# Moving the output gate's projection to block products, and forming the forget gates' low weight halves by adding transfers

## The chip, the cores and the metric

The kernel runs on one core of one Trainium2 chip. The time is the device time of one execution in microseconds (us). The core has five engines that work side by side, each with its own queue in fixed order: TensorE (PE, matrix products into PSUM), VectorE (DVE), ScalarE (ACT), GpSimd (POOL) and SyncE (SP, which here only issues transfers). Transfers between the chip's main memory and the core's memory (SBUF) are issued by SP, ACT or POOL.

## The reference

One layer of a hybrid backbone is applied to 640 tokens of width 1024: 128 context tokens and 512 latent tokens. After a modulation of the input, one wide projection feeds everything:

```python
h = x * (1.0 + scale1) + shift1
proj = h @ p['w_in']
q, f_fwd, f_bwd, i_raw, g_raw, hy, mg = jnp.split(proj, SPLIT_IDX, axis=-1)
o_a, s_f, s_b = hgrn2_mixer(q, f_fwd, f_bwd, i_raw, g_raw, lb, p['hgrn_norm_w'], s0_fwd, s0_bwd)
o_b = hyena_mixer(hy, p, row_len)
```

`hgrn2_mixer` is a gated linear recurrence in both directions over 8 heads of 128 channels. `f_fwd` and `f_bwd` are its forget gates, `i_raw` its values, `g_raw` its output gate:

```python
o = o * lax.rsqrt(jnp.mean(jnp.square(o), axis=-1, keepdims=True) + RMS_EPS) * norm_w.astype(f32)
o = o.reshape(bsz, L, D_A) * jax.nn.silu(g_raw.astype(f32))
```

`hyena_mixer` is a long convolution. Both branches are gated (`mg`), mixed, projected and normalised; a feed-forward block with its own normalisation follows.

## The kernel before

**Two halves of each number.** Each fp32 operand of a large product is split into a rounded high half and the rest, the low half. A product is then three matrix products (`PASSES`): high x high, high x low, low x high. A weight tile of 1024 x 128 is loaded as `raw`, cast on ACT or DVE to the high half `wh`, and the low half `wl` is `raw` minus `wh` (`issue`, line 346; the subtraction is line 358, on DVE, on POOL for some of the first eight tiles). Three buffers each exist for `raw`, `wh` and `wl`, and `advance` (line 361) prepares up to two tiles ahead of the one in use. The strings `HIE` and `LOOK` hold one letter per tile of this stream: the engine of the cast, and how far to look ahead.

**Dense products.** `dense_fm` (line 607) multiplies one 1024 x 128 tile with 320 of the 640 tokens: 8 blocks of the inner dimension x 3 passes. Both halves of the tokens make 48 products of 320 columns for one tile of 128 output channels.

**Block products.** The class `Wino` (line 623) computes two output tiles at once for both token halves by a 2 x 2 block scheme with 7 block products instead of 8. A block product is 4 inner blocks x 3 passes, so a pair costs 84 products instead of 96. In exchange DVE forms sums of weight blocks (`rest`, line 648) and sums of results. In the first projection stage this serves the pairs in `M1_ORDER`: the convolution's `x0`, the mixing gates `mga` and `mgb`, the queries `q` and one pair of forget gates `f`, 14 pairs in all. Its order is written out in `PLAN`: the token `g5` loads and splits the first weight tile of pair 5, `w5` the second one and the sums, `15` to `75` are its seven block products. `m1_done` (line 817) adds the results, applies the gate's function, and stores each finished tile to the scratch `sd` in main memory; line 842 holds a case for an output gate `g`. Tokens `Q` and `Z` put the modulation's own products (`ada`) between them.

**Stages in time.** First the filters and `start`; then the block products, up to about 310 us of the profiled span; then the convolution; then, from about 564 us, the recurrence; then the projection of its output (`pa`), the output product (`wo`), the feed-forward block, and its output (`fo`) to the end.

**The recurrence** follows the order in `HGSEQ`. For head `h`, `a` and `b` are its two forget gates (`hg_f`, line 1146), `q` and `g` its query and output gate, `e` the elementwise part (`hg_elem`, line 1165) and `s` the scan and its norm (`hg_scan`, `hg_post`). `hg_unit` (line 1321) turns each token into a unit of work: a tile that `M1_ORDER` holds is loaded from `sd` (`qg_load`, `f_load`), any other is a dense product with a weight tile from the stream. Seven heads have their forget gates as dense products, all eight their output gates. Between a head's `e` and `s` stand the next head's `a b q g`. The `mga` tiles that are not in `M1_ORDER` come after the last `s` in this order.

`hg_elem` takes the logarithm of the gate on ACT, runs prefix sums on DVE, exponentials on ACT and a row of products on DVE. Its large tiles `t4` to `t7` have one buffer each, as has the gate's own tile `sg` (tag `t1`). `hg_scan` begins with the transposes `kT` on PE, which read the result of these products, then forms scores (`sc`, `scp`), masks them on DVE, and multiplies (`u`, `o`).

The order of instructions in each engine's queue is fixed when the program is built: the library goes by the order in the source and by its own estimate of when an instruction's operands are ready, so that a later piece of work can be placed into a gap. Casts and low halves have priority there.

Of the kernel before, what the change touches and what calls it, by code (L numbers as in the profile page):

```python
# [13 lines left out]
ALU = mybir.AluOpType  # L14
# [3 lines left out]
P = 128  # L18
# [19 lines left out]
COL_Q, COL_FF, COL_FB, COL_I, COL_G = 0, 1024, 2048, 3072, 4096  # L38
# [77 lines left out]
    return {k: np.ascontiguousarray(v) for k, v in c.items()}  # L116


PLAN = """x0 k0 L0 k1 x4 k2 p mlp t L1 T0 x3 T4 A0 x2 D0 T2 A1 x1 L2 B0 M0 T1 D2 A2 M2 T3 h0 L3 B1 D1 A3 h1 B2 M1 D3 h2 h3 M3 h4 W2 W0 h5 h6 h7 W1 q V0 e0 B3 g0 W3 V1 m w0 e2 10 20 g1 50 11 60 g2 70 21 30 40 w1 w2 61 51 52 12 71 Q8 62 22 g3 w3 13 41 g4 53 72 Q9 42 31 63 w4 g5 23 14 w5 73 Z4 Q10 43 32 g6 w6 64 24 15 54 74 Q11 33 65 25 44 16 26 55 75 Q12 Z5 g7 34 w7 66 45 56 17 76 Q13 35 67 46 g8 27 57 w8 18 77 Z6 Q14 g9 g10 36 w9 28 19 68 37 29 58 78 Q15 69 47 59 w10 79 Q16 38 110 210 Z7 g11 610 49 111 510 39 48 w11 211 g12 611 112 w12 212 710 Q17 g13 511 711 Q18 410 113 w13 311 612 Z8 310 411 512 712 Q19 513 213 613 412 713 312 413 313 Z9"""
HMOD = "SVSSVSSS"  # L120
HSUB = "GVVVVGVG"
WSUB = "VGGVVGGG"
# [2 lines left out]
HFE = "VSVSVSVS" * 3 + "VSVSVSVS" + "VSSSVSSS"  # L125
XSE = "S" * 24
M1PRI = 99
M1_ORDER = (('mgb', 6, 7), ('f', 0, 1), ('mgb', 4, 5), ('x0', 6, 7), ('mgb', 2, 3), ('mga', 4, 5), ('x0', 4, 5), ('q', 0, 1), ('q', 2, 3), ('x0', 2, 3), ('q', 6, 7), ('q', 4, 5), ('x0', 0, 1), ('mga', 6, 7))
FFNP = "1-1 2-1 g1 w1"
FFNT = ("g2", "", "")  # L130
FFN0 = "51 61 12 22 w2 71"
PERIOD = (("g", 1), ("w", 1), ("6", 0), ("1", 1), ("4", -1), ("5", 0), ("7", 0), ("3", -1), ("2", 1))
WPRI = 2
HIE = """SSSSVVSVSVSSSSSSSVVVSVVSVSSVSSSSSSSSSSSSSSSSSSSSSSSSSSSSSSSSSSSSSSSSSSSSSSSSSSSSSSSSSSSSSSSSSSSSSSSSSSSSSSSSSS"""
LOOK = """22222012202102201120122111222222222222222222222222222222222222222222222222222222222222222222222222222222222222"""
CONVSEQ = """a0 b0 c0 d0 e0 a1 b1 c1 f0 d1 e1 a2 b2 f1 s04 c2 s00 d2 x0 p0 s01 e2 i00 s02 a3 i01 s03 b3 i02 i03 f2 o00 c3 d3 e3 o01 a4 f3 s14 x1 s10 b4 c4 p1 s11 d4 i10 s12 e4 a5 i11 s13 b5 c5 d5 i12 f4 i13 o10 e5 a6 o11 f5 b6 s24 x2 s20 p2 s21 c6 i20 d6 s22 e6 i21 s23 a7 b7 i22 i23 c7 o20 f6 d7 o21 m0 e7 f7 s34 s30 n0 x3 m1 p3 s31 i30 s32 i31 s33 n1 i32 i33 o30 o31"""
HGSEQ = """a0 b0 q0 g0 e0 v2 v3 a1 b1 q1 g1 s0 e1 a2 b2 q2 g2 s1 e2 a3 b3 q3 g3 s2 e3 a4 b4 q4 g4 s3 e4 a5 b5 q5 g5 s4 e5 a6 b6 q6 g6 s5 e6 a7 b7 q7 g7 s6 e7 s7 c m0 m1 t m2 m3 p0 m4 p1 m5 p2 m6 p3 m7 p4 p5 p6 p7"""
PHB = 2
# [24 lines left out]
def body(tc, I, O):  # L163
    nc = tc.nc
    V, S, G, PE, SY = nc.vector, nc.scalar, nc.gpsimd, nc.tensor, nc.sync
# [3 lines left out]
    def act(out, in_, func, bias=0.0, scale=1.0):  # L169
        r = S.activation(out, in_, func, bias=bias, scale=scale)  # L170
        if func in TABLE_FUNCS:
            if last_table[0] is not None:
                tc.add_manual_dep(
                    r.ins, last_table[0].name,
                    mybir.DependencyInfo(mybir.DependencyClass.NoSync, mybir.DependencyReason.DATA),
                    reason="table order")
            last_table[0] = r.ins
        return r

    def tt(out, a, b, op, eng=None):  # L180
        return (eng or V).tensor_tensor(out=out, in0=a, in1=b, op=op)  # L181
# [4 lines left out]
    def f32(ap):  # L186
        return ap.bitcast(F32)
# [29 lines left out]
    def mm_bank(nm):  # L217
        return bank("mm", nm)
# [20 lines left out]
    w1 = sp.tile([EMB, ORD], F32, name="w1")  # L239
# [12 lines left out]
    w2 = sp.tile([P, ORD], F32, name="w2")  # L252
    w3 = sp.tile([P, 2, ORD], F32, name="w3")
# [84 lines left out]
    stream = dict(specs=[], hl=[], pos=0, stop=None)  # L338

    def w_fm(wap, col):  # L340
        return (wap.rearrange("(k p) n -> p k n", p=P)[:, :, col:col + P], (KT, P), None)

    def w_tm(wap, k0, nk, col, ncol, own=None):
        return (wap.rearrange("(k p) n -> p k n", p=P)[:, k0:k0 + nk, col:col + ncol], (nk, ncol), own)

    def issue(i):
        src, (a, b), own = stream["specs"][i]
        raw = wp.tile([P, a, b], F32, tag="raw", bufs=RAW_BUFS, name=f"raw{i}")
        SY.dma_start(raw, src)
        if own is None:  # L350
            q, th, tl, n = wp, "wh", "wl", HL_BUFS
        else:
            q, th, tl, n = own[0]["p"], "wbh", "wbl", own[1]
        hi = q.tile([P, a, b], F32R, tag=th, bufs=n, name=f"wh{i}")
        lo = q.tile([P, a, b], F32R, tag=tl, bufs=n, name=f"wl{i}")
        with tc.high_priority():
            (V.tensor_copy if HIE[i] == "V" else S.copy)(hi, raw)  # L357
            tt(lo, raw, f32(hi), ALU.subtract, G if i < len(WSUB) and WSUB[i] == "G" else V)
        stream["hl"].append((hi, lo))

    def advance(pos, n):
# [6 lines left out]
        end = len(specs) if stream["stop"] is None else stream["stop"]  # L368
        while ns < end and look < int(LOOK[pos]) and live < HL_BUFS and specs[ns][2] is None:
            ns += 1  # L370
# [15 lines left out]
    def U(fn, *specs):  # L386
        units.append(Unit(list(specs), fn))
# [219 lines left out]
    def dense_fm(w, x, half, ps, kt=KT, after=None):  # L607
        c0 = half * HT
        for k in range(kt):
            for i, (a, b) in enumerate(PASSES):  # L610
                r = PE.matmul(ps[:, 0:HT], w[a][:, k, :], x[b][:, k, c0:c0 + HT],  # L611
                              start=k == 0 and i == 0, stop=k == kt - 1 and i == 2)
                if k == 0 and i == 0:
                    order_after(r, after)
        return r
# [97 lines left out]
    w_in = I["w_in"][0]  # L713
    def v_add(p):
        U(v_unit(p), w_tm(w_in, 0, 4, COL_I + p * 256, 256), w_tm(w_in, 4, 4, COL_I + p * 256, 256))
# [6 lines left out]
    def start():  # L722
# [42 lines left out]

        for tok in PLAN.split():
            if tok == "mlp":
# [9 lines left out]
    M1 = []  # L777
    for kind, a, b in M1_ORDER:
        M1.append(tuple((kind, t) for t in (a, b)))
# [266 lines left out]
    def gate_add(j, tag):  # L1046
        col = COL0[tag] + j * P
        U(gate_unit(j, tag), *(() if (tag, j) in slot else (w_fm(w_in, col),)))
# [73 lines left out]
    def hg_qg(h, which):  # L1122
        def fn(w):
            o = hg["p"].tile([P, T], F32, tag=which, bufs=2 if which == "g" else 1, name=f"{which}{h}")
            for half in range(2):
                cs = slice(half * HT, half * HT + HT)
                ps = mm_bank(f"{which}{h}_{half}")
                dense_fm(w, hT, half, ps)
                act(o[:, cs], ps[:, 0:HT], AF.Sigmoid)
                if which == "g":  # L1130
                    V.scalar_tensor_tensor(o[:, cs], ps[:, 0:HT], norm_w, o[:, cs], ALU.mult, ALU.mult)
                else:
                    tt(o[:, cs], ps[:, 0:HT], o[:, cs], ALU.mult)
            hg[which, h] = o
        return fn

    def qg_load(h, which):
        hg[which, h] = hg["p"].tile([P, T], F32, tag=which, bufs=2 if which == "g" else 1, name=f"{which}{h}")
        spilled(which, h, hg[which, h])

    def f_load(h):
        hg["k", h] = hg["p"].tile([P, 2, T], F32, tag="t1", bufs=1, name=f"sg{h}")
        for d in range(2):
            spilled("f", 2 * h + d, hg["k", h][:, d])

    def hg_f(h, d):
        def fn(w):
            if d == 0:
                hg["k", h] = hg["p"].tile([P, 2, T], F32, tag="t1", bufs=1, name=f"sg{h}")
            o = hg["k", h]  # L1150
            for half in range(2):
                ps = mm_bank(f"f{d}_{h}_{half}")
                dense_fm(w, hT, half, ps)
                act(o[:, d, half * HT:half * HT + HT], ps[:, 0:HT], AF.Sigmoid)
        return fn
# [165 lines left out]
    def hg_unit(tok):  # L1321
        op, h = tok[0], int(tok[1:] or 0)
        if op in "ab":
            d = "ab".index(op)
            if ("f", 2 * h) in slot:
                if d == 0:
                    U(lambda: f_load(h))
                return
            U(hg_f(h, d), w_fm(w_in, (COL_FF, COL_FB)[d] + h * P))
        elif op in "qg":  # L1330
            if (op, h) in slot:
                U(lambda: qg_load(h, op))
            else:
                U(hg_qg(h, op), w_fm(w_in, COL0[op] + h * P))
        elif op == "s":
            U(lambda: (hg_scan(h), hg_post(h)))
        elif op == "e":
            U(lambda: hg_elem(h))
        elif op == "v":
            v_add(h)  # L1340
        elif op == "m":
            gate_add(h, "mga")
        elif op == "p":
            U(proja_unit(h), w_fm(I["proj_a"][0], h * P))
        else:
            U(dict(c=lambda: comb_open(), t=hg_tail)[op])
# [34 lines left out]
    for tok in HGSEQ.split():  # L1381
        hg_unit(tok)
# [402 lines left out]
```

## Time and profile before

| | us |
|---|---|
| median of 3 runs | 1434.0 |
| lowest and highest | 1432.09, 1435.02 |
| the profiled execution | 1434.2 |
| its span | 1431.9 |

A profile is one execution. Its page gives each engine's busy time, the waits, and groups of instructions; the trace behind it can be asked for single instructions. A row of a group reads: line, engine, operation, written tile <- read tiles, shapes, how many | busy us in all, mean ns of one | idle time of the engine just before them, and what ended it. A row of the timeline reads: start, length, engine, line, operation, tiles, shapes, count, and in brackets the engine's idle time before it with what ended it. A row of the stretch view reads: stretch, its length, then for each engine its busy us and the count of its instructions, then the granted share of PE's clock, the busy share of the transfer engines, and GB/s.

```profile
L181 DVE TENSOR_TENSOR wl<-raw,wh 128x1024 fp32r<-128x1024 f32 x96 | 117.3, 1224 | 134.8 <-ACT wh L357 131.2
L357 ACT CAST wh<-raw 128x1024 fp32r<-128x1024 f32 x90 | 94.1, 1049 | 221.8 <-PE pb L611 41.0
```

These two groups are the low halves on DVE (line 181 is the helper `tt` through which most of DVE's two-operand work goes) and the casts on ACT, over the whole kernel. PE's granted clock was 1.00 in every stretch that is quoted below.

### The profile page before, as it was taken

To read this page: it belongs to the slowest core of one execution; us is meant where nothing else is said; L and a number is where in the kernel's file an instruction comes from. 1 tells how busy PE (TensorE), PEld (TensorE's weight loads), DVE (VectorE), ACT (ScalarE), POOL (GpSimd) and SP (SyncE) were. 2 spreads that over 40 slices of the span, in tenths; PEclk is the share of its full clock that TensorE was granted. 3 is DMA by queue.
4 is the path that set the end of the run, shared out by engine and by line. 5 is a ranking of instruction groups with operands and counts; after the bars stand their busy time and mean duration, and the time that the engine had idled before them with its cause. 6 is when DMAs were issued, how large, how long until landed. Compare 5 with 4: busy or idle time off the path is not lost. (4 is left out here: it accounts for less than half of the span.)

```text
span 1431.9 us, 23453 instructions
## 1 busy us (share of the span) xinstructions
PE 1381.0 (96%) x9513; PEld 1293.4 (90%) x9513; DVE 992.3 (69%) x1751; ACT 617.3 (43%) x1011; POOL 64.1 (4%) x56
## 2 busy tenths in 40 slices
PE   4999999999999999999999999999999999999997
PEld 2689889999999989999999999988999898898886
DVE  6886786647889734568788875579976665756426
ACT  3555554433323212455665673337543443442121
POOL 4230000020000000000000000000000000000003
PEclk9999999999999999999999999999999999999999
DMA  7944665674333374422232224632343323357211
GB/s 247 324 141 141 217 216 175 208 244 154 90 100 102 105 230 151 145 74 86 70 95 63 67 67 148 224 103 84 111 119 100 113 82 116 91 182 272 74 60 74
DMA packets 198856, 195.64 MB, mean 137 GB/s; under 512 B 7581, under 2 KB 155773, under 8 KB 197980
## 3 DMA queue, kind: packets, MB, share of 16 engines
q1 hardware_dynamic: 194860, 179.75, 39.9%
q0 software_dynamic: 2160, 9.15, 1.7%
q10 hardware_dynamic: 1728, 5.24, 0.9%
q8 instruction: 74, 1.21, 0.4%
q14 instruction: 34, 0.28, 0.1%
HBM read 162.91 MB, written 31.21 MB: 136 GB/s over the span
## 5 line engine op out<-in xcount | busy, mean ns | idle before, releaser
L181 DVE TENSOR_TENSOR wl<-raw,wh 128x1024 fp32r<-128x1024 f32 x96 | 117.3, 1224 | 134.8 <-ACT wh L357 131.2
L357 ACT CAST wh<-raw 128x1024 fp32r<-128x1024 f32 x90 | 94.1, 1049 | 221.8 <-PE pb L611 41.0
L1423 PE MATMUL fo<-wh,act 128*128 128x512 f32 (+1 forms) x440 | 130.7, 380 | 0.0
L1423 PEld LDWEIGHTS fo<-wh,act 128*128 128x128 f32 x440 | 81.2, 188 | 15.9
L1423 PE MATMUL fo<-wl,act 128*128 128x512 f32 (+1 forms) x220 | 83.4, 379 | 0.0
L611 PE MATMUL hy<-hTh,wh 128*128 128x320 f32 x256 | 79.6, 311 | 0.0
L611 PE MATMUL hy<-hTh,wl 128*128 128x320 f32 x256 | 79.2, 309 | 0.0
L611 PE MATMUL hy<-hTl,wh 128*128 128x320 f32 x256 | 79.1, 309 | 0.0
L611 PE MATMUL f<-hTh,wh 128*128 128x320 f32 x224 | 70.7, 316 | 0.0
L611 PE MATMUL f<-hTl,wh 128*128 128x320 f32 x224 | 69.7, 311 | 0.0
L611 PE MATMUL f<-hTh,wl 128*128 128x320 f32 x224 | 69.2, 309 | 0.0
L181 POOL TENSOR_TENSOR y<-y,gb 128x512 f32<-128x512 f32 x8 | 11.6, 1454 | 908.8 <-ACT y L170 908.5
L1423 PEld LDWEIGHTS fo<-wl,act 128*128 128x128 f32 x220 | 41.3, 188 | 7.9
L611 PEld LDWEIGHTS hy<-hTh,wh 128*128 128x128 f32 x256 | 48.1, 188 | 0.0
L611 PEld LDWEIGHTS hy<-hTl,wh 128*128 128x128 f32 x256 | 48.1, 188 | 0.0
L611 PEld LDWEIGHTS hy<-hTh,wl 128*128 128x128 f32 x256 | 48.1, 188 | 0.0
L707 PE MATMUL v<-wl,hTh 128*128 128x256 f32 x160 | 45.4, 287 | 1.6 <-DVE wl L181 1.6
L170 ACT ACT_TABLE_LOAD x36 | 46.2, 1283 | 1.4 <-PEq L1769 0.7
L707 PE MATMUL v<-wh,hTl 128*128 128x256 f32 x160 | 45.4, 286 | 0.1
L707 PE MATMUL v<-wh,hTh 128*128 128x256 f32 x160 | 45.1, 286 | 0.0
L611 PEld LDWEIGHTS f<-hTl,wh 128*128 128x128 f32 x224 | 42.2, 188 | 0.0
L611 PEld LDWEIGHTS f<-hTh,wh 128*128 128x128 f32 x224 | 42.1, 188 | 0.0
(2291 smaller groups left out, 4708.1 us busy)
## 6 DMA issues: line engine op xcount, KB each, us to landing
raw<-in_w_in SPq DMA_DIRECT2D x52, 512.0 KB, 4.0
rf<-in_ffn_w_in SPq DMA_DIRECT2D x42, 512.0 KB, 4.3
araw<-in_ada_w SPq DMA_DIRECT2D x20, 1024.0 KB, 5.8
rm<-in_w_in SPq DMA_DIRECT2D x28, 512.0 KB, 4.8
raw<-in_ffn_w_out SPq DMA_DIRECT2D x22, 512.0 KB, 5.0
sd<-my SPq DMA_DIRECT2D x28, 320.0 KB, 2.3
kk<-kd SPq DMA_DIRECT2D x20, 256.0 KB, 2.7
ad<-y SPq DMA_DIRECT2D x16, 320.0 KB, 4.4
```

Of the source, the lines that this page charges most:

```text
L170: r = S.activation(out, in_, func, bias=bias, scale=scale)
L181: return (eng or V).tensor_tensor(out=out, in0=a, in1=b, op=op)
L357: (V.tensor_copy if HIE[i] == "V" else S.copy)(hi, raw)
L611: r = PE.matmul(ps[:, 0:HT], w[a][:, k, :], x[b][:, k, c0:c0 + HT], start=k == 0 and i == 0, stop=k == kt - 1 and i == 2)
L707: PE.matmul(ps[:, (t - t0) * 256:(t - t0) * 256 + 256], hT[b][:, k, t * P:t * P + P], w[a][:, k % 4, :], start=k == 0 and i == 0, stop=k = ...
L1423: PE.matmul(ps, x(t, b, k0 + kk), w[a][:, kk, :], start=first and kk == 0 and i == 0, stop=last and kk == nk - 1 and i == 2)
```

## The change

It has two parts.

The eight tiles of the output gate go to the block products. `M1_ORDER` gets four pairs of them at its end, and `PLAN` the tokens for pairs 14 to 17, between and behind the last tokens of pairs 12 and 13. In `hg_unit` the output gate is now found in `slot`, so that each head loads it from `sd` instead of multiplying. The scratch `sd` grows by eight tiles. `HIE` and `LOOK` lose eight letters, all of them "S" and "2", from the end of the stream, where all letters are the same.

The low halves of the 14 forget-gate tiles that are still dense products are formed in another way. ACT writes the negative of `raw`, rounded, to `wl`, and POOL issues a transfer that reads the same weights once more from main memory and adds them to `wl` as it writes. What is left is again the weight minus its rounded value.

```diff
-M1_ORDER = (('mgb', 6, 7), ('f', 0, 1), ('mgb', 4, 5), ('x0', 6, 7), ('mgb', 2, 3), ('mga', 4, 5), ('x0', 4, 5), ('q', 0, 1), ('q', 2, 3), ('x0', 2, 3), ('q', 6, 7), ('q', 4, 5), ('x0', 0, 1), ('mga', 6, 7))
+M1_ORDER = (('mgb', 6, 7), ('f', 0, 1), ('mgb', 4, 5), ('x0', 6, 7), ('mgb', 2, 3), ('mga', 4, 5), ('x0', 4, 5), ('q', 0, 1), ('q', 2, 3), ('x0', 2, 3), ('q', 6, 7), ('q', 4, 5), ('x0', 0, 1), ('mga', 6, 7), ('g', 0, 1), ('g', 2, 3), ('g', 4, 5), ('g', 6, 7))
...
+    adding = set()
+
     def issue(i):
...
             (V.tensor_copy if HIE[i] == "V" else S.copy)(hi, raw)
-            tt(lo, raw, f32(hi), ALU.subtract, G if i < len(WSUB) and WSUB[i] == "G" else V)
+            if id(stream["specs"][i]) in adding:
+                S.mul(lo, raw, -1.0)
+                G.dma_start(lo, src, accum_op=ALU.add)
+            else:
+                tt(lo, raw, f32(hi), ALU.subtract, G if i < len(WSUB) and WSUB[i] == "G" else V)
         stream["hl"].append((hi, lo))
...
-            U(hg_f(h, d), w_fm(w_in, (COL_FF, COL_FB)[d] + h * P))
+            spec = w_fm(w_in, (COL_FF, COL_FB)[d] + h * P)
+            adding.add(id(spec))
+            U(hg_f(h, d), spec)
```

The end of `PLAN`, after the token `Q19` that both have, before and after:

```
513 213 613 412 713 312 413 313 Z9

213 g14 w14 613 114 412 513 713 312 214 Z9 g15 w15 614 115 413 514 714 313 215 g16 w16 615 116 414 515 715 314 216 g17 w17 616 117 415 516 716 315 217 617 416 517 717 316 417 317
```

More of the change, by code (lines that the diff above doesn't have):

```diff
@@ L116, in _constants @@
     return {k: np.ascontiguousarray(v) for k, v in c.items()}
-PLAN = """x0 k0 L0 k1 x4 k2 p mlp t L1 T0 x3 T4 A0 x2 D0 T2 A1 x1 L2 B0 M0 T1 D2 A2 M2 T3 h0 L3 B1 D1 A3 h1 B2 M1 D3 h2 h3 M3 h4 W2 W0 h5 h6 h7 W1 q V0 e0 B3 g0 W3 V1 m w0 e2 10 20 g1 50 11 60 g2 70 21 30 40 w1 w2 61 51 52 12 71 Q8 62 22 g3 w3 13 41 g4 53 72 Q9 42 31 63 w4 g5 23 14 w5 73 Z4 Q10 43 32 g6 w6 64 24 15 54 74 Q11 33 65 25 44 16 26 55 75 Q12 Z5 g7 34 w7 66 45 56 17 76 Q13 35 67 46 g8 27 57 w8 18 77 Z6 Q14 g9 g10 36 w9 28 19 68 37 29 58 78 Q15 69 47 59 w10 79 Q16 38 110 210 Z7 g11 610 49 111 510 39 48 w11 211 g12 611 112 w12 212 710 Q17 g13 511 711 Q18 410 113 w13 311 612 Z8 310 411 512 712 Q19 513 213 613 412 713 312 413 313 Z9"""
+PLAN = """x0 k0 L0 k1 x4 k2 p mlp t L1 T0 x3 T4 A0 x2 D0 T2 A1 x1 L2 B0 M0 T1 D2 A2 M2 T3 h0 L3 B1 D1 A3 h1 B2 M1 D3 h2 h3 M3 h4 W2 W0 h5 h6 h7 W1 q V0 e0 B3 g0 W3 V1 m w0 e2 10 20 g1 50 11 60 g2 70 21 30 40 w1 w2 61 51 52 12 71 Q8 62 22 g3 w3 13 41 g4 53 72 Q9 42 31 63 w4 g5 23 14 w5 73 Z4 Q10 43 32 g6 w6 64 24 15 54 74 Q11 33 65 25 44 16 26 55 75 Q12 Z5 g7 34 w7 66 45 56 17 76 Q13 35 67 46 g8 27 57 w8 18 77 Z6 Q14 g9 g10 36 w9 28 19 68 37 29 58 78 Q15 69 47 59 w10 79 Q16 38 110 210 Z7 g11 610 49 111 510 39 48 w11 211 g12 611 112 w12 212 710 Q17 g13 511 711 Q18 410 113 w13 311 612 Z8 310 411 512 712 Q19 213 g14 w14 613 114 412 513 713 312 214 Z9 g15 w15 614 115 413 514 714 313 215 g16 w16 615 116 414 515 715 314 216 g17 w17 616 117 415 516 716 315 217 617 416 517 717 316 417 317"""
 HMOD = "SVSSVSSS"
@@ L133 @@
 WPRI = 2
-HIE = """SSSSVVSVSVSSSSSSSVVVSVVSVSSVSSSSSSSSSSSSSSSSSSSSSSSSSSSSSSSSSSSSSSSSSSSSSSSSSSSSSSSSSSSSSSSSSSSSSSSSSSSSSSSSSS"""
-LOOK = """22222012202102201120122111222222222222222222222222222222222222222222222222222222222222222222222222222222222222"""
+HIE = """SSSSVVSVSVSSSSSSSVVVSVVSVSSVSSSSSSSSSSSSSSSSSSSSSSSSSSSSSSSSSSSSSSSSSSSSSSSSSSSSSSSSSSSSSSSSSSSSSSSSSS"""
+LOOK = """222220122021022011201221112222222222222222222222222222222222222222222222222222222222222222222222222222"""
 CONVSEQ = """a0 b0 c0 d0 e0 a1 b1 c1 f0 d1 e1 a2 b2 f1 s04 c2 s00 d2 x0 p0 s01 e2 i00 s02 a3 i01 s03 b3 i02 i03 f2 o00 c3 d3 e3 o01 a4 f3 s14 x1 s10 b4 c4 p1 s11 d4 i10 s12 e4 a5 i11 s13 b5 c5 d5 i12 f4 i13 o10 e5 a6 o11 f5 b6 s24 x2 s20 p2 s21 c6 i20 d6 s22 e6 i21 s23 a7 b7 i22 i23 c7 o20 f6 d7 o21 m0 e7 f7 s34 s30 n0 x3 m1 p3 s31 i30 s32 i31 s33 n1 i32 i33 o30 o31"""
```

## The prediction

> **What bounds the kernel now.** I read the page's busy line first, then the waits of TensorE (PE), then two stages in the stretch view, then the timeline of the one place where PE waits in the second of them.
>
> ```profile
> span 1431.9 us, 23453 instructions
> PE 1381.0 (96%) x9513; PEld 1293.4 (90%) x9513; DVE 992.3 (69%) x1751; ACT 617.3 (43%) x1011; POOL 64.1 (4%) x56
> ...
> 859.10 56.33 PE pa L611 x384
> ```
>
> PE is busy for 96% of the span. The third line, from the chain, prices a dense product: 56.33 us / 384 = 0.1467 us each. The profiled execution took 1434.2 us around its 1431.9 us span, against a median of 1434.0; I sum against 1434.2.
>
> The first projection stage ends in this stretch (all work; line 668 alone; the `ada` products alone; columns: stretch, its length, busy PE, PEld, DVE, ACT, POOL as far as they work):
>
> ```profile
> 258.99:309.85 50.86, 50.70 (x347) 47.08 (x345) 33.78 (x61) 24.64 (x43) 5.11 (x2) 1.00 0.62 191
> 258.99:309.85 50.86, 47.46 (x314) 45.70 (x312) 1.00 0.62 191
> 258.99:309.85 50.86, 3.20 (x24) 0.50 (x24) 1.17 (x2) 1.00 0.62 191
> 120.00:160.00 40.00, 39.49 (x262) 36.04 (x261) 26.08 (x38) 21.80 (x39) 0.00 (x0) 1.00 0.64 198
> ```
>
> PE is idle for 0.16 us of 50.86; an earlier stretch, the last row, is the worst of the stage with 0.51 of 40. Besides 314 block products there are 24 `ada` products (3.20 us) and 9 small transposes (about 1 us, an estimate at the 0.11 us of the transposes below). So a block product takes (50.86 - 3.20 - 1.0) / 314 = 0.1486 us.
>
> In the recurrent stage the heads follow each other. A period runs from one head's `kT` transposes to the next head's:
>
> ```profile
> 776.25:807.93 31.68, 31.68 (x280) 31.23 (x278) 26.13 (x44) 19.69 (x30) 0.00 (x0) 1.00 0.24 70
> 807.93:835.10 27.17, 25.78 (x240) 25.10 (x239) 22.85 (x39) 18.97 (x29) 0.00 (x0) 1.00 0.17 49
> PE kT L1232 <- DVE t L181: 1.4, 1, 1.4
> 807.93 1.03 PE L1232 MATMUL kT<-cst,t 128*128 128x128 f32 x8
> 833.11 0.63 PE L1232 MATMUL kT<-cst,t 128*128 128x128 f32 x4 [1.39 <-DVE t L181]
> 835.38 0.63 PE L1232 MATMUL kT<-cst,t 128*128 128x128 f32 x4
> ```
>
> This is the row that decides my forecast. Six periods (head 0 to head 6) look like the first row: three dense weight tiles (two forget gates, one output gate) beside the scan, 31.68 us, PE never idle. The last period has two dense tiles (`mga`), because no head 8 follows. There PE runs dry: 27.17 us, of which 1.39 us idle before the first four `kT`. The change gives the six other periods two tiles as well.
>
> **The change, part by part.**
>
> *The product count.* Eight output-gate tiles leave the recurrent stage: 8 x 48 = 384 dense products x 0.1467 = 56.3 us of PE. Four pairs join the first stage: 4 x 7 x 12 = 336 block products x 0.1486 = 49.9 us. On PE alone: **-6.4 us**. Everything below asks how much of it stays.
>
> *The first stage's other engines.* One output-gate pair takes PE 84 x 0.1486 = 12.5 us. These rows have the shapes of its VectorE (DVE) work (the first and last are of the later feed-forward products, which share the code):
>
> ```profile
> L181 DVE TENSOR_TENSOR rf<-rf,rf 128x512 f32<-128x512 f32 x20 | 13.8, 688 | 0.3
> L181 DVE TENSOR_TENSOR wl<-raw,wh 128x1024 fp32r<-128x1024 f32 x30 | 36.7, 1223 | 42.6 <-ACT wh L357 42.6
> L1131 DVE SCALAR_TENSOR_TENSOR g<-g,prT,g x16: 505/546/555, 564.6 to 810.2; 128x320 f32<-128x320 f32 x16
> L181 DVE TENSOR_TENSOR fu<-fc,fu 128x320 f32<-128x320 f32 x15 | 7.0, 485 | 0.2 <-PE fc L668 0.2
> ```
>
> DVE makes four sums of 128x512 (2.75), low halves of three 512-wide and two 1024-wide operands (2.06 + 2.45), three output sums (1.46) and four norm products (2.18): 10.9 us of 12.5. It fits under PE, so I add nothing; at the idle share of the stage's worst stretch, 0.51 of 40, the pairs would cost 0.6 us more in all. SP gets eight stores and eight loads of 320 KB in place of eight weight loads (the weights now go through line 633, also 8 x 512 KB), in a stretch whose DMA share is 0.62; ACT gets 16 sigmoids more in the first stage and 16 fewer later. I count these at nothing, hidden under PE. The loads of gate `g` join SP's queue behind weight loads; those run two tiles ahead, so an SP wait of a few us reaches nobody. The first two output-gate tiles run before head 0's scan, outside the six periods, where PE isn't held by this loop; their share of the gain is whole.
>
> *The recurrent period.* PE needs 31.68 - 48 x 0.1467 = 24.64 us. Does the other chain fit in that? It is the loop `kT` of one head, logarithm on ACT (its output tile has one buffer, which `kT` must have read), then DVE nearly without a gap to the product that feeds the next `kT`:
>
> ```profile
> 826.06 1.49 DVE L181 TENSOR_TENSOR t<-t,q 128x1280 f32<-128x1280 f32 x1 [0.95 <-ACT t L170]
> 827.47 1.48 DVE L181 TENSOR_TENSOR t<-t,sg 128x1280 f32<-128x1280 f32 x1
> 828.87 1.22 DVE L181 TENSOR_TENSOR wl<-raw,wh 128x1024 fp32r<-128x1024 f32 x1
> 830.00 1.49 DVE L181 TENSOR_TENSOR t<-t,sg 128x1280 f32<-128x1280 f32 x1
> ...
> 834.41 0.82 DVE L181 TENSOR_TENSOR t<-t,ff 128x640 f32<-128x640 f32 x1
> 824.75 2.44 ACT L170 ACTIVATE t<-t 128x1280 f32<-128x1280 f32 x2
> 827.09 1.04 ACT L357 CAST wh<-raw 128x1024 fp32r<-128x1024 f32 x1
> 828.03 1.27 ACT L170 ACTIVATE t<-t 128x1280 f32<-128x1280 f32 x1
> ...
> 636.96 1.04 ACT L357 CAST wh<-raw 128x1024 fp32r<-128x1024 f32 x1
> 795.41 1.04 ACT L357 CAST wh<-raw 128x1024 fp32r<-128x1024 f32 x1
> ```
>
> The second four `kT` start at 835.38, right after the product that ends at 834.41 + 0.82; the second four of the head before started near 808.37 (half of the 0.87 us from 807.93 to the 808.81 of what follows). The chain is 27.0 us. PE had 24.64 us of work of its own in it and used 25.78: about 1.1 us was work of a later tile, placed early, which is not lost; 1.39 us was lost. So with two tiles a period loses **1.39 us**, if the chain stays as it is.
>
> *The low halves by transfer.* Fourteen subtractions of 1.22 us leave DVE; fourteen ACT passes arrive, and fourteen transfers issued from POOL. An ACT pass over 128x1024 isn't in the trace with a scale; the nearest rows are the cast (1.04) and, scaled from 1280 columns, the exponential (1.27 x 0.8 = 1.02). I take 1.04, 0.94 from start to start. Only one subtraction per period stands in the chain (828.87, 1.13 from start to start). Its removal frees DVE at 828.87, but the next product needs the exponential that ended about 829.3: gain 0.7. If the new ACT pass stands right behind the cast at 827.09, as both become ready when a weight buffer comes free, that exponential ends at 830.2 and the product starts 0.2 later than before. So the chain changes by **-0.7 to +0.2 us** a period. Behind the pass on ACT wait the exponential and, through it, DVE. Weights are prepared two tiles ahead, so the last three preparations in these six periods are for `mga` tiles with ordinary subtractions, and about 4.5 periods are touched: -3.2 to +0.9 us. I take 0, nearer to the upper end, since the casts of three periods (the last two rows, and 827.09) all stood between the exponentials.
>
> *The transfer's landing* must be bounded from its neighbours:
>
> ```profile
> raw<-in_w_in SPq DMA_DIRECT2D x52, 512.0 KB, 4.0
> itl<-in_itl POOLq DMA_DIRECT2D x1, 1152.0 KB, 10.3
> 502.33 2.25 POOL L397 DMA_DIRECT2D araw<-in_ada_w  x3 [9.74 <-DVE ob L181]
> ```
>
> POOL issues in 0.75 us and is idle in this stage, so nothing queues behind it. The landing lies between 4.0 (the same bytes, plain) and, read and written back, twice 10.3 = 20.6. The cast is released when the tile three places ahead in the stream is done, so the low half is due one tile, one scan and one tile later: 7.04 + 10.56 + 7.04 = 24.6 us. Cast, pass and issue take 2.8; so 21.8 are left, over both ends. Cost nothing; beyond 21.8 us PE would wait. [...]
>
> *Sum.* -6.4 + 6 x 1.39 = +1.9; 1434.2 + 1.9 = **1436.1 us**. Ends: -1.3 (all of the chain's gain) to +3.4 (0.9, and the 0.6 of the first stage).
>
> **The rivals.**
>
> *PE stays the bound.* The chain falls below 24.6 us, and all 6.4 us remain: 1427.8. For it: DVE drops from 26.1 us a period by 3.7 (three subtractions) and 1.1 (two norm products) to 21.3, well under 24.6. Against it: the last period had only 22.85 us of DVE and yet lost 1.39. It needs 2.4 us off a chain of 27.0, and I find 0.7.
>
> *Slower: nothing is placed early.* In the last period 1.1 us of the 2.5 us gap was filled with `mga` products. In the others the next forget gate must fill it, whose sigmoid waits for a one-buffer tile until DVE has read it, while four PSUM banks hold its halves. If the fill fails, each period is 27.17 against 24.64: 6 x 2.53 = 15.2, net +8.8: 1443.0. It decides from the point where the chain exceeds 24.64 + 1.39 us. For it: the exponential's 0.95 us wait grows if the pass falls ahead of it. Against: the order that filled the last period.
>
> *A late low half.* With a landing of 25 us, the alternate tile (seven) would each be 3.2 us late: +22, near 1458. The other seven have a scan more of time. It decides at 21.8 us; no row comes near. [...]
>
> *The change doesn't do what it says:* if no tile is recognised as adding, the subtractions stay, as in the measured last period: +1.9 again, told apart only by the count of subtractions.
>
> **How the numbers follow.** Forecast case 42%, within 1432.9 to 1437.6; PE-bound, or most of the way there, 22%; nothing filled 30%; late half 4%; not done 2%. The range reaches to 1428 (PE-bound nearly whole) and 1443 (nothing filled), leaving about 15% out. Against a median of 1434.0, 0.2% is 2.9 us, about what a measurement of this kernel can tell from no change. Faster by more: the PE-bound case and a little: 24%. Slower by more: nothing filled, late halves and the top of my own case: 36%. Within: 40%.
>
> **What would show it.** Block products 1176 + 336; dense `g` products gone. Six periods between `kT` transposes near 26.0 us (24.64 if PE is the bound, 27.2 if nothing is filled), each with one PE wait on DVE `t`. Subtractions `wl` in this stage about 8 instead of 30. An ACT pass right behind a cast between the exponentials, and DVE waiting there. No PE wait on a transfer. I am wrong if the periods show no wait of PE, or if the added pairs in the first stage run above 0.15 us a product.

## The result, and the profile after

The changed kernel takes **1454.35 us** (median of 4 runs, 1449.09 to 1457.34) against 1434.1 us: ratio 1.0148, 95% interval 1.0132 to 1.0163. The forecast was 1436.1, with a range of 1428 to 1443: about no change, where the kernel is 1.5% slower, 18 us above the forecast and 11 above the range. The profiled execution took 1454.9 us, with a span of 1453.1.

The head of the page, and the waits of TensorE (PE) from the first forget tile to the last head:

```profile
span 1453.1 us, 23507 instructions
PE 1381.9 (95%) x9465; PEld 1291.8 (89%) x9465; DVE 1001.7 (69%) x1777; ACT 641.1 (44%) x1049; POOL 85.0 (6%) x70
...
PE kT L1238 <- DVE t L181: 11.3, 6, 2.8
PE pa L617 <- ACT mga L170: 2.7, 1, 2.7
PE f L617 <- DMA wl<-in_w_in: 2.3, 1, 2.3
PE mga L617 <- ACT mga L170: 1.7, 1, 1.7
```

PE's busy time has hardly changed (1381.0 before), though 6 us of products left it: part of what remains runs slower, as shown below. Before, PE waited once for `kT` in this stage (1.4 us); now it waits six times, 11.3 us, and three times for other things.

I cut both spans at the same instructions. All times are us from one profiled execution each; `e1`, `e5`, `e6` are experiments described below (gate move alone; adding transfers from head 2 on; gate move with the ScalarE pass but no transfer).

| stretch | before | after | e1 | e5 | e6 |
|---|---|---|---|---|---|
| start to the first `hy` product | 309.85 | 358.91 | 359.59 | 357.04 | 359.04 |
| to the last `v` product | 286.99 | 280.29 | 280.27 | 280.33 | 280.32 |
| to head 0's second four `kT` | 21.39 | 18.50 | 14.36 | 14.36 | 14.36 |
| to head 7's second four `kT` (seven periods) | 217.15 | 194.04 | 187.11 | 194.03 | 194.07 |
| to the first `wo` product | 79.89 | 82.64 | 79.88 | 81.30 | 81.26 |
| to the end | 516.63 | 518.72 | 517.99 | 519.74 | 517.95 |
| span | 1431.9 | 1453.1 | 1439.2 | 1446.8 | 1447.0 |

The first row comes from the same code in the four changed kernels and still varies by 2.5 us, so a difference of that size between two single profiles says little.

The first row is also the price of the moved tiles: +49.06 for 336 block products, 0.146 each, PE never idle in the added stretch, as this row shows (columns as in the prediction):

```profile
309.85:358.91 49.06, 49.06 (x336) 49.06 (x335) 35.55 (x67) 19.67 (x40) 4.98 (x2) 1.00 0.49 156
```

What comes back is 6.7 in the second row, 2.9 in the third instead of 7.0, and 23.1 in the seven periods instead of some 34. Three periods of after and the end of one of them:

```profile
684.04:710.91 26.87, 26.59 (x238) 25.52 (x239) 21.79 (x40) 20.38 (x31) 3.22 (x3) 1.00 0.67 140
738.57:766.18 27.61, 24.83 (x232) 24.15 (x231) 21.87 (x40) 19.79 (x30) 2.70 (x3) 1.00 0.63 134
766.18:796.36 30.18, 27.39 (x239) 26.71 (x238) 24.31 (x43) 19.19 (x29) 2.72 (x2) 0.94 0.55 111
791.43:795.43 4.00, 4.00 (x20) 4.00 (x21) 4.00 (x7) 1.75 (x5) 0.00 (x0) 0.65 0.29 44
```

The typical period is 27.6 us, not 26.0. The third is 30.2. Its granted clock (the third number from the end) is 0.65 for four us after a wait, which costs some 1.4 us, and it holds seven products more (239 against 232), another 1.0 us.

### The profile page after: what moved, and what is told of

Read it like the earlier page. It is cut to its first block, busy times and chain, and to the rows that moved or that the text cites. A ratio compares the mean times of both kernels' runs of the same rounds, so it can differ in the third digit from the quotient of the medians.

```text
span 1453.1 us, 23507 instructions
## 1 busy us (share of the span) xinstructions
PE 1381.9 (95%) x9465; PEld 1291.8 (89%) x9465; DVE 1001.7 (69%) x1777; ACT 641.1 (44%) x1049; POOL 85.0 (6%) x70
## 4 chain that ended last, share of the span: by engine, by line
PE 64%; DVE 11%; DMA 10%; ACT 8%; issue 4%; POOL 1%; SPq 1%; DVEq 0%; ACTq 0%; POOLq 0%
PE fo L1431 10%; PE hy L617 8%; PE ma L674 6%; DMA rf<-in_ffn_w_in 6%; PE pa L617 4%; PE pb L617 4%; PE wo L1431 4%; PE mc L674 3%; PE f L617 3%; PE v L713 2%; DMA rm<-in_w_in 2%; PE fw L980 2%; DVE rf L181 2%; PE inv L1015 2%; PE fa L674 2%
## 5 line engine op out<-in xcount | busy, mean ns | idle before, releaser
L359 ACT CAST wh<-raw 128x1024 fp32r<-128x1024 f32 x82 | 85.6, 1048 | 192.1 <-PE pb L617 41.0
L181 DVE TENSOR_TENSOR wl<-raw,wh 128x1024 fp32r<-128x1024 f32 x74 | 90.3, 1223 | 92.4 <-ACT wh L359 91.4
L181 POOL TENSOR_TENSOR y<-y,gb 128x512 f32<-128x512 f32 x8 | 11.6, 1452 | 647.3 <-ACT y L170 647.0
L617 PEld LDWEIGHTS f<-hTh,wl 128*128 128x128 f32 x224 | 43.4, 194 | 2.6 <-DMA wl<-in_w_in 2.6
```

## Experiments

**First four: the two halves of the change apart, and two other ways to make a low half.** Theory A was a chain through VectorE (DVE) and ScalarE (ACT) that ends last with two dense tiles a period, lengthened by the pass; theory B, that the adding transfers are nearly the whole loss.

e1, gate move alone:

```
-            adding.add(id(spec))
```

> The changed kernel without adding transfers: all low halves of the forget tiles by VectorE's subtraction again, the gate tiles stay in the first stage. Theory A (with two dense tiles a period the chain through ScalarE and VectorE ends last; the ScalarE pass lengthens it by some 0.6 us a period, and the late first low halves cost 4.0): periods near 27.1 us, no wait in the first forget tile, 1454.35 - 4.0 - 7 x 0.55 = 1446.5 us (1444 to 1449), so still slower than before. Theory B (the adding transfers are nearly the whole loss): 1428 to 1436. Theory C (they cost nothing): 1452 to 1456.

Measured: 1440.66 us, ratio 1.0061 (1.0046 to 1.0076), below A's range and above B's.

e2, adding transfers alone, the kernel before with these lines and the branch in `issue`:

```
+            spec = w_fm(w_in, (COL_FF, COL_FB)[d] + h * P)
+            adding.add(id(spec))
```

> The kernel before with the adding transfers alone: the gate tiles stay dense. Theory A: six periods stay at 31.7 us, because TensorE has 7 us of work more in each than the chain has; what remains is the first forget tile's late low halves (+4.0) and the last period (+0.6): 1438 us (1434 to 1441). Theory B: the loss stays with the transfers, 1448 to 1455.

Measured: 1442.18 us, ratio 1.0072 (1.0055 to 1.0088), above A's range and below B's.

Each half costs 8 to 10 us; neither theory has it all. A steady period of e1:

```profile
734.29:761.05 26.76, 25.45 (x231) 24.27 (x232) 23.97 (x42) 17.92 (x27) 0.00 (x0) 1.00 0.34 99
```

26.76 us each time, where PE's own work is 24.64: a period loses 2.1 us and not 1.39. Compare its dense products (line of tile `f`) with those of the last period of before (tile `mga`), cut at the same instruction, the second four `kT`:

```profile
734.29:761.05 26.76, 15.76 (x97) 14.34 (x97) 0.00 (x0) 1.55 (x4) 1.00 0.34 99
808.37:835.38 27.01, 16.23 (x101) 14.92 (x101) 0.00 (x0) 1.10 (x3) 1.00 0.17 49
```

Two tiles are 96 products, and one more is cut by the edge of each row. So before held four products of a later tile, 0.6 us, where I had counted 1.1 us as early work that is not lost. In a row of equal periods whatever is placed early is missing from the next one, so only the length of the chain counts: 27.0 us there, 26.76 here. PE is idle for 1.31 us of e1's period; the other 0.8 us is busy time beyond 24.64, whose cause isn't shown. DVE is busy for 23.97 of 26.76.

In e2 head 1's second forget tile, the second tile with an adding transfer, shows the transfer by itself (a wait of PE, the four us that follow, and a period):

```profile
L617 PE MATMUL f<-hTh,wl 128*128 128x320 f32 x216 | 67.6, 313 | 4.3 <-DMA wl<-in_w_in 4.3
607.80:611.80 4.00, 3.94 (x16) 3.94 (x17) 0.00 (x0) 0.00 (x0) 0.00 (x0) 0.57 1.24 268
655.42:687.67 32.25, 31.95 (x281) 31.24 (x280) 24.02 (x42) 21.53 (x33) 3.13 (x2) 1.00 0.57 122
```

PE waits 4.3 us for the low half and then runs at a clock of 0.57: 27.53 us from the last `v` product to head 0's second four `kT` instead of 21.39. Of the six periods four are 32.25 instead of 31.69; there PE waits 1.2 us for ACT's sigmoids in all.

e3, the low half subtracted on GpSimd (POOL), and e4, the pass on POOL:

```
-                S.mul(lo, raw, -1.0)
-                G.dma_start(lo, src, accum_op=ALU.add)
+                tt(lo, raw, f32(hi), ALU.subtract, G)
```

```
-                S.mul(lo, raw, -1.0)
+                G.tensor_scalar(lo, raw, -1.0, None, ALU.mult)
```

> The changed kernel with the 14 low halves subtracted on GpSimd (2.54 us each by the rows of its other subtractions) in place of the ScalarE pass and the adding transfer. Theory A: both the pass (1.05 us) and the subtraction (1.13 us) are out of the chain, the periods go to some 26.2 us and the late first halves go: 1454.35 - 4.0 - 7 x 1.5 = 1440 us (1436 to 1444). Theory B (TensorE is the bound once no transfer is late): periods 24.7, 1427 to 1432. If a subtraction of 2.54 us is itself late for its products: above 1446.

> The changed kernel with the pass times -1 on GpSimd in place of ScalarE; the adding transfers stay. Theory A: the pass leaves the chain, periods near 26.6 us, the first tile's late low halves stay: 1454.35 - 7 x 1.05 = 1447 us (1443 to 1450). Theory B (it is the transfers' lateness, not the pass): 1452 to 1457, with TensorE waiting on the transfer.

Measured: e3 1468.69 us (1.026, 1.0242 to 1.0277), e4 1449.19 us (1.0126, 1.0107 to 1.0144). e4 is in A's range: without the pass ACT gives back 5 us. But its periods are 26.4 to 28.9 us and not 26.6 each; there one DVE product (`t<-t,q`) takes 2.12 us beside POOL's pass in five heads, against 1.49 in e1. e3 falls outside both theories. It lies where the third case has it, a subtraction late for its products, but not for that reason: PE never waits for POOL's `wl` there. The groups of three periods, DVE's product in e1 and in e3, and below it PE's wait for `kT` in e3's stage (a subtraction takes POOL 2.69 us there):

```profile
L181 DVE TENSOR_TENSOR t<-t,sg 128x1280 f32<-128x1280 f32 x8 | 11.9, 1484 | 0.0
```

```profile
L181 DVE TENSOR_TENSOR t<-t,sg 128x1280 f32<-128x1280 f32 x7 | 17.4, 2488 | 1.5 <-ACT t L170 1.5
PE kT L1237 <- DVE t L181: 25.4, 13, 3.6
```

The mean of 2488 ns hides two sizes. DVE's timeline of one period of e3, and the clock over its recurrence:

```profile
739.50 1.48 DVE L181 TENSOR_TENSOR t<-t,sg 128x1280 f32<-128x1280 f32 x1
741.37 3.24 DVE L181 TENSOR_TENSOR t<-t,sg 128x1280 f32<-128x1280 f32 x1 [0.39 <-ACT t L170]
640.00:843.00 203.00, 178.99 (x1550) 173.47 (x1552) 151.03 (x236) 116.62 (x175) 34.99 (x13) 0.94 0.27 81
```

POOL's subtraction starts at 740.24. The product that already runs keeps its 1.48 us; the next one, which starts beside it, takes 3.24. A subtraction of 1.13 us taken off DVE so comes back as 1.76 us more on another DVE product of the chain, and one of these periods takes 31.56 us. Behind four of the longer waits the granted clock is 0.50 to 0.62 over four us; over the stage it is 0.94, at most 12 us of e3's loss (0.06 x 203; in e1 it is 1.00 there).

**Next four: pass and transfer apart.**

e5, adding from head 2 on, so that only head 1's tiles are subtracted:

```
+            if h > 1:
                 adding.add(id(spec))
```

> The changed kernel with the adding transfers from head 2 on only; head 1's two low halves are subtracted on VectorE. If the first tile's late low half costs what its stage shows (18.06 against 13.92 us, the clock at 0.57 for 4 us in it included): 1454.35 - 4.1 = 1450 us (1448 to 1452). If that stall only takes the place of a later one: 1453 to 1456.

e6, the pass without the transfer, and e7, a transfer without the pass:

```
                 S.mul(lo, raw, -1.0)
-                G.dma_start(lo, src, accum_op=ALU.add)
```

```
-                S.mul(lo, raw, -1.0)
-                G.dma_start(lo, src, accum_op=ALU.add)
+                G.dma_start(lo, src)
```

> The changed kernel without the adding transfer: the ScalarE pass alone, so that the low halves are the negated weights and the sums are others than the reference's. Theory P (the pass stands in the chain of exponentials, 0.85 us a period, and makes waits of 2.5 us behind which the clock halves): periods stay at 27.6, the first tile's wait goes, 1447 to 1452. Theory T (the transfer itself, its landing or its issue, makes the loss): periods at 26.8 or less, 1438 to 1443.

> The changed kernel with a plain transfer of the weights into the low half on the same queue in place of pass and adding transfer, so that the sums are others than the reference's: no ScalarE pass and no subtraction. Theory P: the periods fall below the 26.76 us of the kernel with the gate move alone, by up to the 1.13 us of the subtraction (25.6 to 26.8); the first low halves stay somewhat late: 1434 to 1443. Theory T: 27.5 and more, 1448 to 1456.

Measured: e5 1449.51 us (1.0119, 1.01 to 1.0138), e6 1450.65 us (1.0125, 1.0104 to 1.0145), e7 1440.05 us (1.005, 1.0034 to 1.0066). Theory P: **the pass alone makes e5's whole time, and a transfer without it costs no more than the subtraction that it replaces** (e1, 1440.66). e5 and e6 agree to 0.04 us in the seven periods (table). e7 has no subtraction on DVE either, and its steady periods are 26.24 us.

The rest of the transfer's cost is one late low half, that of head 1's second tile: 4.1 us between after and e5 in the third row of the table, 4.8 between the medians. Its cast waited for a buffer that a `v` product held, and its transfer landed 8.8 us after it was issued, when PE had waited 2.35 us:

```profile
637.72 1.05 ACT L359 CAST wh<-raw 128x1024 fp32r<-128x1024 f32 x1 [0.78 <-PE v L713]
640.03 1.56 POOL L362 DMA_DIRECT2D wl<-in_w_in  x1 [9.78 <-ACT wl L361]
648.88 0.41 PE L617 MATMUL f<-hTh,wl 128*128 128x320 f32 x1 [2.35 <-DMA wl<-in_w_in]
```

Where the pass hurts is seen by laying ACT's timeline of after and of e1 side by side. After, with DVE's two rows beneath:

```profile
754.94 1.27 ACT L170 ACTIVATE t<-t 128x1280 f32<-128x1280 f32 x1
756.12 1.03 ACT L359 CAST wh<-raw 128x1024 fp32r<-128x1024 f32 x1
757.06 1.06 ACT L361 ACTIVATE wl<-raw 128x1024 fp32r<-128x1024 f32 x1
758.02 2.42 ACT L170 ACTIVATE t<-t 128x1280 f32<-128x1280 f32 x2
...
763.07 1.04 ACT L359 CAST wh<-raw 128x1024 fp32r<-128x1024 f32 x1
764.00 1.06 ACT L361 ACTIVATE wl<-raw 128x1024 fp32r<-128x1024 f32 x1
...
756.25 1.49 DVE L181 TENSOR_TENSOR t<-t,q 128x1280 f32<-128x1280 f32 x1 [0.96 <-ACT t L170]
759.30 2.89 DVE L181 TENSOR_TENSOR t<-t,sg 128x1280 f32<-128x1280 f32 x2 [1.56 <-ACT t L170]
```

e1:

```profile
750.42 2.44 ACT L170 ACTIVATE t<-t 128x1280 f32<-128x1280 f32 x2
752.76 1.04 ACT L359 CAST wh<-raw 128x1024 fp32r<-128x1024 f32 x1
753.71 1.27 ACT L170 ACTIVATE t<-t 128x1280 f32<-128x1280 f32 x1
```

In e1 the cast stands behind two of the three exponentials. After, cast and pass stand behind one: DVE's second product waits 1.56 us for its exponential. DVE's busy time falls (21.87 against 23.97) and the period still grows by 0.85. The next cast and its pass (763.07, 764.00) stand ahead of three of the head's four sigmoids `sg` and of the copies of `kT`; in e1 that cast stands behind three sigmoids (at 758.25) and has no pass behind it.

e8, the first pair of gate tiles moved, nothing else:

```
-... ('mga', 6, 7))
+... ('mga', 6, 7), ('g', 0, 1))
```

> The kernel before with only the first two gate tiles moved to the first stage's block products, no adding transfers. These two lie ahead of the six periods, where no chain takes back what TensorE saves: the stage grows by a quarter of the measured 49.06 us, 12.3, and 2 x 7.04 us go: 1432.55 - 1.8 = 1430.8 us (1429 to 1432). If the period that follows has its own wait there (its exponentials no longer hidden behind a gate tile): 1433 to 1437.

Measured: 1435.46 us over 12 runs, 1.0015 (1.0005 to 1.0026). The first stage grew by 13.58 us (first `hy` product at 323.43), more than the 12.3 expected, against 2 x 7.04; the spans, 1431.8 and 1431.9, say a draw. The time lies in the second option's range, but its reason doesn't hold: the six periods stay at 31.69 us. That it came out a little slower in the median I can't explain from its profile.

**Then: is it really the chain?** If so, shortening it must make the gate move pay. Three edits: the rescaled gate on ACT, the state copies on ACT, and one exponential of each head formed as a product.

```
-            V.tensor_scalar(kk[:, d], kk[:, d], noml[:, pc], oml[:, pc], ALU.mult, ALU.add)
+            act(kk[:, d], kk[:, d], AF.Identity, bias=oml[:, pc], scale=noml[:, pc])
...
-            V.tensor_copy(ns, ps[:, 384:512])
+            S.copy(ns, ps[:, 384:512])
```

```
-            tt(ck(t2[:, d]), bt[:, 0, d] ..., ck(t3[:, d]), ALU.subtract)
...
-        act(t2, t2, AF.Exp)
+        act(eb, bt[:, 0], AF.Exp)
...
-        tt(t2, t2, kk, ALU.mult)
+        tt(t2 by chunks, t5 by chunks, eb broadcast, ALU.mult)
```

e9 is e1 with the first two edits; e10 the kernel before, e11 e1 and e12 the changed kernel with all three.

> The kernel with the gate move alone (no adding transfers), and two short VectorE operations of each head on ScalarE instead: the rescaled gate kk (2 x 0.61 us) and the copy of the new state (2 x 0.28 us). If VectorE's queue sets the period (24.2 us busy of 26.76): the periods shrink by 1.2 to 1.8 us towards TensorE's 24.64, 1440.66 - 7 x 1.2 = 1432 us (1429 to 1435). If ScalarE's exponentials set it: no gain or a loss, 1440 to 1446.

> The kernel before with those two moves and, besides, exp(b0 - t3) formed as the product of exp(-t3)*kk and exp(b0), which takes 1.64 us of VectorE and one exponential of 1.27 us out of each head; nothing else changed. Six periods are TensorE's 31.69 us there, so only the last period (27.0) can shrink: 1433.5 - 1.5 = 1432 us (1430 to 1434). If the periods of before were bound by VectorE or ScalarE after all: 1425 or less.

> The gate move alone with all three of these edits. If the chain through VectorE and ScalarE is what kept the gate move from paying, the periods now reach TensorE's 24.64 us: 1440.66 - 7 x 2.0 = 1426.7 us (1424 to 1430), faster than before. If something else holds the periods: 1433 or more.

> The changed kernel (gate move and adding transfers) with all three edits. If the pass costs only as a link of the chain, and the half clock only behind its waits of 2.5 us: periods near 24.7 to 25.3, the first tile's late low halves stay, 1432 us (1429 to 1437). If pass or transfer cost by themselves (ports, queues): 1441 or more.

| kernel | us | ratio to before, 95% | period, us |
|---|---|---|---|
| e9: gate move, two edits | 1430.16 | 0.9971 (0.9959 to 0.9983) | 24.97 |
| e10: before, three edits | 1435.61 | 1.0008 (0.9999 to 1.0018) | 32.0 |
| e11: gate move, three edits | 1429.63 | 0.9969 (0.9957 to 0.9981) | 24.98 |
| e12: whole change, three edits | 1442.82 | 1.0055 (1.0041 to 1.007) | 26.46 |

A period of e9, with PE idle for 0.11 us of it:

```profile
703.71:728.68 24.97, 24.86 (x233) 24.21 (x231) 22.24 (x38) 19.51 (x32) 0.00 (x0) 1.00 0.28 80
```

The chain theory holds: the same three edits give nothing where PE is the bound (e10) and 11 us where the gate move has made the chain the bound (e11 against e1). e9 and e11 are faster than before by 0.3%. The rest of the product count's 6.4 us is partly spent on PE itself, which needs 0.3 us a period more with these edits. That is also why e10 lies above its range: its last period falls from 27.01 to 23.07 us, but the six others take 32.0 instead of 31.69, and the work behind them takes longer too.

e12 misses: the adding transfers cost 13 us against e11 even on the short chain (6.6 between the two profiled spans, of which e12's was its fastest run). In it PE waits at another place, and ACT's queue shows the pass again:

```profile
PE msp L1301 <- ACT sqh L1298: 6.0, 5, 1.2
...
734.85 1.05 ACT L359 CAST wh<-raw 128x1024 fp32r<-128x1024 f32 x1 [2.94 <-PE f L617]
735.80 1.05 ACT L361 ACTIVATE wl<-raw 128x1024 fp32r<-128x1024 f32 x1
```

The cast waits 2.94 us at the head of ACT's queue for PE to free its buffer; the pass stands right behind it, ahead of the sigmoid and the copies of `kT` that begin the next head. Those are on the chain whatever DVE does. This is read from the row; no run moves the pass within e12.

**Last: place or time, and which edit.** e14 issues the pass and the transfer behind the block of high priority and not in it:

```
         with tc.high_priority():
             (V.tensor_copy if HIE[i] == "V" else S.copy)(hi, raw)
-            if id(stream["specs"][i]) in adding:
-                S.mul(lo, raw, -1.0)
...
+        if id(stream["specs"][i]) in adding:
+            S.mul(lo, raw, -1.0)
+            G.dma_start(lo, src, accum_op=ALU.add)
```

e13 is e1 with the first edit (rescaled gate) alone, e15 with the second (copies) alone.

> The changed kernel with the ScalarE pass and the adding transfer issued in their plain order and not ahead of waiting work (the cast keeps its place). If the pass costs by its place in ScalarE's queue, between the exponentials and before the state's copies: the periods fall towards 26.8 us and only the first tile's late low halves stay: 1441 to 1447. If it costs by ScalarE's time wherever it stands, or if the low half is now late for its products: 1450 to 1458.

> The gate move alone with only the rescaled gate kk on ScalarE (1.22 us of VectorE's queue a head); the state copies are VectorE's again. If 1.2 us off the chain is enough and the state copies on ScalarE were what kept the periods at 24.97 us: 24.64 us each, 1430.16 - 7 x 0.33 = 1428 us (1426 to 1430). If the copies' 0.56 us of VectorE was needed as well: periods of 25.2 to 25.6, 1432 to 1435.

> The gate move alone with only the two state copies of each head on ScalarE; the rescaled gate stays on VectorE. With the rescaled gate alone moved, the wait of 1.34 us a period went from the transposes to the small sums of squares, which wait for a ScalarE cast behind an exponential. If the copies alone bring the order that avoids this wait: 1429 to 1432, as with both. If both are needed (the copies for the order, the rescaled gate for VectorE's time): periods of 26 us and more, 1436 to 1441.

Measured: e14 1444.83 us (1.0066, 1.0046 to 1.0085), e13 1440.38 us (1.0042, 1.0029 to 1.0054), e15 1438.1 us (1.0039, 1.0025 to 1.0052).

e14's periods with adding settle at 26.24 us, shorter than e1's 26.76, since a subtraction has left DVE and the pass now stands behind the exponentials. Here is one of these periods, one of e7, which has no pass at all, and the place of the pass in e14:

```profile
713.37:739.61 26.24, 24.98 (x231) 24.23 (x231) 21.89 (x40) 19.82 (x30) 3.10 (x2) 1.00 0.59 116
707.92:734.16 26.24, 24.86 (x231) 24.21 (x231) 21.89 (x40) 17.96 (x27) 1.75 (x2) 1.00 0.50 116
729.64 2.44 ACT L170 ACTIVATE t<-t 128x1280 f32<-128x1280 f32 x2
731.98 1.04 ACT L359 CAST wh<-raw 128x1024 fp32r<-128x1024 f32 x1
732.92 1.27 ACT L170 ACTIVATE t<-t 128x1280 f32<-128x1280 f32 x1
...
735.08 1.04 ACT L363 ACTIVATE wl<-raw 128x1024 fp32r<-128x1024 f32 x1
```

ACT is busy for 1.86 us more than in e7, and the period is the same. So **the pass costs by its place, not by its time**. What is left is the late low half of head 1's second tile (20.48 us for the third row of the table, against 14.36).

e13 missed. With the rescaled gate on ACT, PE no longer waits for `kT`, and waits as long for the small sums of squares:

```profile
PE msp L1301 <- ACT sqh L1298: 1.3, 1, 1.3
```

```profile
745.33 1.27 ACT L170 ACTIVATE t<-t 128x1280 f32<-128x1280 f32 x1
746.51 0.39 ACT L1298 CAST sqh<-sq 128x256 fp32r<-128x256 f32 x1
```

The second rows are ACT's: an exponential, ready earlier now, has gone ahead of the cast `sqh`, whose product stands in PE's queue in front of the forget tile's. In e15 the periods are 26.32, as expected if both edits are needed, and the wait is `kT`'s again. Each edit alone leaves a wait of 1.3 us a period; both together leave none.

## Why the prediction was wrong, step by step

- **The product count** was right: predicted +49.9 in the first stage, measured +49.06; 2 x 7.04 us go ahead of head 0 when nothing else disturbs (6.7 and 7.0 in e1). The first stage's other engines cost nothing, as said.
- **The loss of 1.39 us a period is the step that failed first.** Its working took the 1.1 us of early work in before's last period as not lost. That period borrowed from the work that follows the loop, once; six periods in a row can't. The working also contradicts itself: it kept the chain at 27.0 us and set the period at 26.0, shorter than the chain that closes it. e1 shows 26.76 us with the products of two tiles and no more: the loss is about 2.1 a period, 12.5 in six (the time from head 0 to head 6, 160.35 us, less 6 x 24.64), not 8.3. With -6.4 that is +6.1; e1's span has +7.3. The rival "nothing is placed early" had this mechanism, at 30%; by its own condition, a chain over 26.03 us, it was the case already at the chain of 27.0.
- **The chain's -0.7 to +0.2 us for the pass is the step that failed most.** I took the cast's place, behind two exponentials, as given, and placed the pass behind it. In the changed kernel both stand behind one exponential, a second cast and pass stand ahead of the copies of `kT`, and PE waits for the following `mga` tiles too (2.7 and 1.7 us). Instead of 0 it is some 8 to 10 us (e6 against e1: spans of 1447.0 and 1439.2, medians of 1450.65 and 1440.66): 7.0 in the seven periods, 1.4 behind them, the rest within what two profiles differ by. I had named DVE's wait for the exponential as what the profile would show, but bounded it by one order of ACT's queue.
- **The landing, "hidden", "decides at 21.8".** In the steady periods that held: the median landing is 7.1 us, between my ends of 4.0 and 20.6, and PE waits for no transfer there. At the head of the stage the step was never worked out. The weights of head 1's second forget tile wait for a buffer that a `v` tile still holds, and there the lead of one tile, one scan and one tile doesn't exist. Cost: 4.1 to 4.8 us (after against e5). The rival "a late low half" had the right wait and the wrong place.
- **The clock wasn't in the sum at all.** Waits of 2.35, 2.79 and 2.66 us were followed by a lower clock in three places of the profiled execution (0.57, 0.65 and 0.50 over four us): 1.7 and 1.4 us lost in the four us at 0.57 and 0.65, and `pa` at 59.18 us instead of 56.33. That is 6 us together, part of it inside the costs named above, and most of why PE's busy time didn't fall (it is 1377.3 in e1). The four runs of after spread over 8 us, with mean clocks from 0.988 (1457.34 us) to 0.994 (1449.09 us).
- **"POOL issues in 0.75 us"**: an adding transfer took 1.56 us to issue. Nothing queued behind it, so it cost only landing.

Added up, 1436.1 + 4.2 (12.5 in place of 8.3) + 8 to 10 (the pass) + 4.1 to 4.8 (the late low half) gives 1452 to 1455, against the measured 1454.35.

Two us at the end of the span (518.72 against 516.63) lie mostly in unchanged feed-forward code; of those I haven't found the cause.

## What to carry to other kernels

Where a loop of equal periods loses its bound engine's work, take the length of the next chain as the new period; work that a last or single period fills in from outside isn't there for the others. When an operation moves to another engine, ask first behind and ahead of what it will stand in that engine's queue, and look at the first period, where buffers come free late, separately. To make such a move pay, first shorten the chain that it uncovers: here two short operations on ScalarE turned +0.6% into -0.3%.

## What the runs showed of the hardware

**Behind five of the waits quoted here, of 2.15 to 4.3 us, TensorE's granted clock was 0.50 to 0.66 over the next four us; behind others, of 1.69 to 2.78 us, it was 1.00.** The wait of 4.3 us, with 0.57 behind it, is that of e2 above. The stretches of four us after PE's waits in after, of 2.35, 2.49, 2.78, 2.79 and 2.66 us:

```profile
648.87:652.87 4.00, 3.99 (x17) 3.99 (x18) 0.00 (x0) 0.00 (x0) 1.15 (x1) 0.57 1.33 237
736.19:740.19 4.00, 4.00 (x32) 4.00 (x33) 3.67 (x7) 3.68 (x8) 1.55 (x1) 1.00 0.65 141
763.81:767.81 4.00, 4.00 (x32) 4.00 (x33) 3.67 (x7) 3.68 (x8) 1.55 (x1) 1.00 0.62 132
...
875.20:879.20 4.00, 4.00 (x15) 4.00 (x16) 2.69 (x3) 3.12 (x6) 0.00 (x0) 0.50 0.16 47
```

The fourth, at 791.43, is quoted further up (0.65). Behind two more waits of after, of 2.52 and 1.69 us, it stayed at 1.00. The unchanged wait of 2.15 us ahead of the feed-forward stage shows the same in before, and in e1 the clock behind it stayed at 1.00:

```profile
987.60:991.60 4.00, 4.00 (x19) 4.00 (x20) 4.00 (x8) 4.00 (x9) 0.00 (x0) 0.66 0.00 2
```

The waits of 1.3 to 1.4 us in the recurrence of e7, e13 and e15 showed no such effect: the granted clock is 1.00 from 640 to 850 us in e7, and in seven stretches of four us behind such waits in each of e13 and e15. The length of the wait alone doesn't sort the places: behind 2.35 us the clock was 0.57, behind 2.49, 2.52 and 2.78 us 1.00, and behind the unchanged wait ahead of the feed-forward stage 0.66 in before and 1.00 in e1. What decides it, these runs don't show.

**An adding transfer** of 512 KB took 1.56 us to issue and 7.1 us from issue to landing (median of 14; 8.8 to 11.7 for the first four); the plain transfer of the same bytes from the same queue in e7 5.9, and from SyncE's queue 3.9:

```profile
L362 POOL DMA_DIRECT2D wl<-in_w_in x14 | 21.8, 1556 | 212.4 <-ACT wl L361 115.5 <-ACT xx L170 75.2 <-ACT sg L170 16.4
wl<-in_w_in POOLq DMA_DIRECT2D x14, 512.0 KB, 7.1
```

Beside VectorE's two-operand products an issue took 1.55 to 1.57 us (the first of all 1.61), no longer than where VectorE did nothing: three of them took 4.66 us there (the row below), 1.55 each.

```profile
638.97:657.70 18.73, 16.39 (x103) 16.11 (x103) 0.00 (x0) 7.74 (x11) 4.66 (x3) 0.91 1.10 218
```

**GpSimd beside VectorE.** In e3 a VectorE product of 128x1280 that started beside a GpSimd subtraction of 128x1024 took 3.24 us instead of 1.48; one that was already running when the subtraction started kept its 1.48.
